# Strassen products that accumulate in PSUM banks, in a two-layer hybrid decoder step

## Chip, core and metric

The kernel runs on one core of a Trainium2 chip. The metric is the device time of one execution in microseconds (us). TensorE multiplies matrices into PSUM banks, VectorE and ScalarE do elementwise work, GpSimd does elementwise work on SBUF alone, and SyncE issues the DMAs. Each engine works through its own queue in order.

## What is computed

One inference step for 512 prompt tokens and 64 sample tokens, through two layers of width 1024. The part that matters here, per layer:

```
h = RMSNorm(x);  P = h @ W_in            # columns: four mixers and four merge-gate blocks G_b
o_b = mixer_b(P_b)                       # HGRN2, GLA, RWKV-7, retention, 256 wide each
x = x + W_out( sum_b sigmoid(G_b) * (o_b @ W_branch[b]) )
g, u = split(RMSNorm(x) @ W_ffn_in)      # 2 x 2816 columns
x = x + (silu(g) * u) @ W_ffn_out
```

Inputs and outputs are float32. The 576 tokens are handled in two halves of 288 (HW). Features lie on the partitions, tokens along the free axis.

## The kernel before

Every float32 operand of a large product is split into two float16 parts, hi and lo. A product of a 128 x 128 weight block with 288 tokens is then three matmuls, hi·hi, hi·lo and lo·hi, into one PSUM bank. To split a weight, ScalarE writes the hi part and VectorE then the lo part (`strassen_weights`, L1692 and L1693; for ordinary products `wload`, L228 and L229).

Two stages use Strassen's scheme in Winograd's form, with seven products of quarter size in place of eight: the merge gates of the last two branches (`last_gates`, eight pairs of feature tiles per layer) and 19 of the 22 feature tiles of the feed-forward's input product (`ffn`, from tile 3 on; one tile of g and one of u together). A is the weight block (rows: two feature tiles; columns: halves of the contraction), B the tokens:

```
S1 = A21 + A22, S2 = S1 - A11, S3 = A22 - S2, S4 = A12 - S2     (GpSimd, L1696)
P1 = A11 B11, P2 = A12 B21, P3 = S4 B22, P4 = A22 T4, P5 = S1 T1, P6 = S2 T2, P7 = S3 T3
U2 = P1 + P6, U3 = U2 + P7, U4 = U2 + P5
C = [[P1 + P2, U4 + P3], [U3 + P4, U3 + P5]]
```

Each product is 12 matmuls (L1718 to L1720), 84 for a tile or a pair. `strassen` (L1708) runs A11, A12, A22, S2, S1, S3, S4, each into a PSUM bank of its own. ScalarE copies P1 to SBUF (L1739). Then seven VectorE additions (L1734), each with one addend in PSUM and one in SBUF, form U2, U4, U3 and the four quarters of C: tiles su and sc. In the feed-forward, ScalarE takes Silu of a quarter of g (L1763), VectorE multiplies it with the quarter of u (L1765, tile fy), and the result is split (L248, L250) into fa. In the merge gates, ScalarE takes Tanh of each quarter (L1529), and after all seven products four up-projections of six matmuls each (tile ub, L1537) follow; VectorE multiplies (L1539, tile gu), GpSimd adds into mg (L1540), and for the last branch mg is split into mh (L252).

The PSUM has eight banks in three rings: b (four), g (two), r (two). A tile of a ring waits until an earlier tile of that ring has had its last reader. During the first four pairs of a layer's merge gates the RWKV-7 recurrence (tiles rws, rtk, ryn, rw_o) runs in between.

The program is written as generators that are stepped in turn; a scheduler then orders the instructions of each engine, and tiles get their memory as they come free. GpSimd works with VectorE on the weights: the sum for S2 needs A11's lo part made first, since it overwrites A11.

Of the kernel before, what the change touches and what calls it, by code (L numbers as in the profile page):

```python
# [62 lines left out]
def host_constants():  # L63
    """Arrays that depend on shapes alone."""
# [110 lines left out]
class Net:  # L175
# [14 lines left out]
    def t(self, ring, shape, name, dt=F32):  # L190
        """A tile of a ring: tiles of one ring get their memory in the program's order."""
# [41 lines left out]
    def gemm(self, ps, w, ks, c0, m, rhs, step=4):  # L233
        """ps[m, :] = sum over k of w(k)^T rhs(k), both in float16 parts. Yields within, after every step products."""
# [10 lines left out]
    def split(self, out_hi, out_lo, src, scale=1.0):  # L245
        """src * scale = hi + lo in float16."""
# [61 lines left out]
    def first_norm(self, half):  # L308
        """x transposed and stored, and its norm, for half the tokens, from the rows of x."""
# [25 lines left out]
    def setup(self):  # L335
        """The other constants."""
# [44 lines left out]
        # lower bounds of HGRN2's forget gates: softmax over depth, cumulated, minus the first  # L381
# [11 lines left out]
        self.lb = cp.tile([128, 2, 2, 2], F32, name="lb")  # [layer, (lb, 1 - lb), tile]  # L393
# [4 lines left out]
        # buffers with zeros off their diagonal blocks that stay  # L398
# [18 lines left out]
    def chunk_sums(self, out, x, mask):  # L417
        """Sums along the tokens that start anew at each chunk's and each sample's first token."""
# [18 lines left out]
    def rstd(self, half):  # L437
        """1 / rms of each token of a half, on all partitions."""
# [50 lines left out]
    def silu_evac(self, dst, scale):  # L489
        """dst = silu(p * PH) * scale."""  # L490
# [1452 lines left out]
```

## Time and profile before

| what | value |
|---|---|
| three runs | 2266.75, 2272.84 (median), 2273.5 us |
| profiled execution, span | 2268.2 us (no other time is listed for it) |
| TensorE busy | 2056.5 us, 91% |
| VectorE busy | 1704.2 us, 75% |
| ScalarE busy | 1070.3 us, 47% |
| GpSimd busy | 693.5 us, 31% |
| merge gates in Strassen's form | about 538 to 692 us, and 1651 to 1805 us |
| feed-forward products in Strassen's form | about 796 to 1009 us, and 1906 to 2121 us |

A share over the whole span is a mean of stages that have different limits, so it is read by stage. The start of a ScalarE copy of P1 (tile sp) marks the end of a tile's first product; the distance between such copies is the period of a tile.

### The profile page before, as it was taken

The page shows a single profiled execution, that of the slowest core. Times are in us where ns is not written, and L with a number is a line of the kernel's source. Part 1 is how long each engine was busy: PE and PEld are TensorE (multiplying, and loading weights), DVE is VectorE, ACT ScalarE, POOL GpSimd, SP SyncE. Part 2 cuts the span into 40 slices and gives each one's busy share as a digit, 9 for nine tenths or more (in the row PEclk, how much of TensorE's full clock was granted, in tenths as well). Part 3 has the DMA queues.
Part 4 walks back from the last instruction along what each step waited for, and adds up shares of the span by engine and source line. Part 5 has one row for each costly group of instructions (what it writes and reads, how often), then busy time and mean ns, then how long its engine had stood idle before and what let it go on. Part 6 is the DMA issues. An engine that isn't in the chain of part 4 may idle for free. (4 is left out here: it accounts for less than half of the span.)

```text
span 2268.2 us, 42128 instructions
## 1 busy us (share of the span) xinstructions
PE 2056.5 (91%) x15754; PEld 1622.1 (72%) x15754; DVE 1704.2 (75%) x3719; ACT 1070.3 (47%) x2400; POOL 693.5 (31%) x850
## 2 busy tenths in 40 slices
PE   7988899997889898999999889889988988989998
PEld 5766776786667676777777667768766766767776
DVE  7899766768786799973388997686688768998532
ACT  6554545346444554442365344363544455444432
POOL 2212212135650555430012121212375416544000
PEclk9999999998999999999999999999999999999999
DMA  6312223322226133234321222242333352232331
GB/s 176 81 36 65 57 57 89 93 72 80 81 80 197 52 88 94 66 117 119 114 71 48 58 54 61 53 111 71 80 88 86 106 155 70 81 89 75 118 109 50
DMA packets 365721, 195.42 MB, mean 86 GB/s; under 512 B 58946, under 2 KB 359546, under 8 KB 365516
## 3 DMA queue, kind: packets, MB, share of 16 engines
q1 hardware_dynamic: 365516, 192.73, 30.3%
q8 instruction: 124, 2.03, 0.4%
q14 instruction: 81, 0.66, 0.1%
HBM read 173.72 MB, written 16.59 MB: 84 GB/s over the span
## 5 line engine op out<-in xcount | busy, mean ns | idle before, releaser
L241 PE MATMUL pb<-h,whl 128*128 128x288 f16 (+1 forms) x1504 | 440.2, 293 | 3.7 <-ACT h L463 2.2
L243 PE MATMUL pb<-h,whl 128*128 128x288 f16 (+1 forms) x1504 | 440.4, 293 | 2.5 <-DVE whl L229 2.5
L242 PE MATMUL pb<-h,whl 128*128 128x288 f16 (+1 forms) x1504 | 440.3, 293 | 0.6 <-DVE h L464 0.4
L229 DVE SCALAR_TENSOR_TENSOR whl<-raw,whl 128x512 f16<-128x512 f32 (+1 forms) x352 | 252.0, 726 | 129.3 <-ACT whl L228 127.6
L242 PEld LDWEIGHTS <-whl 128*128 128x128 f16 (+1 forms) x2784 | 276.9, 99 | 92.0 <-issue 16.1
L243 PEld LDWEIGHTS <-whl 128*128 128x128 f16 (+1 forms) x2784 | 277.4, 100 | 88.8 <-issue 11.9
L241 PEld LDWEIGHTS <-whl 128*128 128x128 f16 (+1 forms) x2784 | 279.3, 100 | 77.1 <-issue 3.6
L228 ACT ACTIVATE whl<-raw 128x512 f16<-128x512 f32 (+1 forms) x352 | 212.8, 616 | 166.7 <-PE pb L243 57.5
L243 PE MATMUL xb<-fa,whl 128*128 128x288 f16 x704 | 201.3, 286 | 0.0
L242 PE MATMUL xb<-fa,whl 128*128 128x288 f16 x704 | 201.3, 286 | 0.0
L241 PE MATMUL xb<-fa,whl 128*128 128x288 f16 x704 | 201.3, 286 | 0.0
L1696 POOL TENSOR_TENSOR sraw<-sraw 128x512 f32<-128x512 f32 x80 | 119.5, 1496 | 70.3 <-DVE hA L1693 34.0
L1718 PE MATMUL fsA<-h,hA 128*128 128x288 f16 x432 | 125.4, 290 | 13.3 <-DVE gu L1539 10.8
L1718 PE MATMUL fsS<-st,hS 128*128 128x288 f16 x456 | 131.3, 288 | 6.4 <-ACT hS L1692 6.4
L1720 PE MATMUL fsS<-st,hS 128*128 128x288 f16 x456 | 131.2, 288 | 0.9 <-DVE hS L1693 0.9
L1719 PE MATMUL fsS<-st,hS 128*128 128x288 f16 x456 | 131.1, 288 | 0.0
L1720 PE MATMUL fsA<-h,hA 128*128 128x288 f16 x432 | 125.4, 290 | 5.1 <-DVE hA L1693 5.1
L1719 PE MATMUL fsA<-h,hA 128*128 128x288 f16 x432 | 125.5, 290 | 0.0
L1696 POOL TENSOR_TENSOR raw<-raw 128x512 f32<-128x512 f32 x52 | 80.1, 1540 | 130.0 <-DVE hA L1693 100.8
L1693 DVE SCALAR_TENSOR_TENSOR hA<-sraw,hA 128x512 f16<-128x512 f32 x110 | 108.2, 992 | 9.8 <-ACT hA L1692 9.7
L1718 PEld LDWEIGHTS <-hS 128*128 128x128 f16 x864 | 85.6, 99 | 34.8 <-ACT hS L1692 12.9
L1719 PEld LDWEIGHTS <-hA 128*128 128x128 f16 x648 | 63.9, 99 | 60.3 <-issue 44.7
(486 smaller groups left out, 5325.4 us busy)
## 6 DMA issues: line engine op xcount, KB each, us to landing
raw<-in_w_in SPq DMA_DIRECT2D x208, 256.0 KB
sraw<-in_w_ffn_in SPq DMA_DIRECT2D x40, 512.0 KB
raw<-in_w_ffn_out SPq DMA_DIRECT2D x80, 256.0 KB
raw<-in_w_ffn_in SPq DMA_DIRECT2D x78, 256.0 KB
x<-xd SPq DMA_DIRECT2D x32, 288.0 KB
sraw<-in_w_in SPq DMA_DIRECT2D x32, 256.0 KB
raw<-in_w_out SPq DMA_DIRECT2D x32, 256.0 KB
xd<-x SPq DMA_DIRECT2D x48, 144.0 KB
```

The lines of the kernel that those rows point to most:

```text
L228: nc.scalar.activation(hl[:, 0, :n], raw[:, :n], AF.Copy, scale=WS)
L229: nc.vector.scalar_tensor_tensor(hl[:, 1, :n], raw[:, :n], WS, hl[:, 0, :n], op0=MUL, op1=SUB)
L241: nc.tensor.matmul(ps, wh, hi, start=i == 0, stop=False)
L242: nc.tensor.matmul(ps, wh, lo, start=False, stop=False)
L243: nc.tensor.matmul(ps, wl, hi, start=False, stop=i == len(ks) - 1)
L1693: nc.vector.scalar_tensor_tensor(hl[:, 1], a, WS, hl[:, 0], op0=MUL, op1=SUB)
L1696: nc.gpsimd.tensor_tensor(dst, a, b, op=op)
L1718: nc.tensor.matmul(ps, w[a][:, 0, k], hi, start=k == 0, stop=False)
L1719: nc.tensor.matmul(ps, w[a][:, 0, k], lo, start=False, stop=False)
L1720: nc.tensor.matmul(ps, w[a][:, 1, k], hi, start=False, stop=k == 3)
```

## The change

P6 and P7 are no longer put into banks of their own. P1 is made in a bank X; ScalarE copies it out as p1, P6 (S2) is accumulated onto it (X is then U2, copied as u2), then P7 (S3; X is U3, copied as u3), and in the next pair's turn P4 (A22; X is then a finished quarter). P5 (S1) is made in a bank Z, and P3 (S4) is accumulated onto it in the next pair's turn. P2 (A12) has a bank Y. Three VectorE additions remain: p1 + Y, u3 + Z, u2 + Z. ScalarE makes three copies, not one. A pair's order is A11, the older pair's A22, S1, the older pair's S4, S2, A12, S3. What follows a quarter (Silu, product and split, or Tanh, up-projection and sum) comes as each quarter is finished. The weights' splits are reordered to suit, and are made further ahead.

```diff
@@ strassen_weights
-        for name, a, op0, op1 in (("A11", a11, a21, a11), ("A22", a22, a22, a11), ("A12", a12, a12, a11)):
-            split(name, a)
-            add(a, op0, op1, SUB)
-            yield
-        for name, a in (("S2", a11), ("S1", a21), ("S3", a22), ("S4", a12)):
-            split(name, a)
-            yield
+        split("A11", a11)
+        add(a11, a21, a11, SUB)
+        yield
+        split("S1", a21)
+        yield
+        split("S2", a11)
+        yield
+        split("A22", a22)
+        add(a22, a22, a11, SUB)
...
@@ strassen
-        def plus(a, p, name):
-            o = self.t(ring if name[1] == "c" else "gt", [128, HW], name)
-            nc.vector.tensor_tensor(o, a, p, op=ADD)
...
-        p1 = self.t("gt", [128, HW], "sp1")
-        nc.scalar.copy(p1, (yield from product("b", "A11", b(0, h0))))
-        c11 = plus(p1, (yield from product("b", "A12", b(4, h0))), "sc11")
-        p4 = yield from product("g", "A22", tt(3))
-        u2 = plus(p1, (yield from product("b", "S2", tt(1))), "su2")
-        p5 = yield from product("g", "S1", tt(0))
-        u4 = plus(u2, p5, "su4")
-        u3 = plus(u2, (yield from product(ps3, "S3", tt(2))), "su3")
-        c22 = plus(u3, p5, "sc22")
-        c21 = plus(u3, p4, "sc21")
-        c12 = plus(u4, (yield from product(ps3, "S4", b(4, h1))), "sc12")
+        def kept(ring, ps, name):
+            o = self.t(ring, [128, HW], name)
+            nc.scalar.copy(o, ps)
+            return o
+        def plus(a, ps):
+            nc.vector.tensor_tensor(a, a, ps, op=ADD)
+            return a
+        old = None
+        for key in [*keys, None]:
+            new = key is not None
+            if new:
+                rx, rz, ry, rc = rings(key)
+                prep(key, 0)
+                x = self.psum(rx, [128, HW], "fsX")
+                yield from product(key, "A11", x, b(0, h0), True)
+                p1 = kept(rc, x, "sp1")
+                prep(key, 1)
+            if old:
+                okey, ox, oz, ou2 = old
+                yield from product(okey, "A22", ox, lambda k: tt(okey, 3, k), False)
+                yield from then(okey, 2, ox)
+            if new:
+                prep(key, 2)
+                z = self.psum(rz, [128, HW], "fsZ")
+                yield from product(key, "S1", z, lambda k: tt(key, 0, k), True)
+                prep(key, 3)
+            if old:
+                yield from product(okey, "S4", oz, b(4, h1), False)
+                yield from then(okey, 1, plus(ou2, oz))
+            if new:
+                prep(key, 4)
+                yield from product(key, "S2", x, lambda k: tt(key, 1, k), False)
+                u2 = kept(rc, x, "su2")
+                prep(key, 5)
+                y = self.psum(ry, [128, HW], "fsY")
+                yield from product(key, "A12", y, b(4, h0), True)
+                yield from then(key, 0, plus(p1, y))
+                prep(key, 6)
+                yield from product(key, "S3", x, lambda k: tt(key, 2, k), False)
+                u3 = kept(rc, x, "su3")
+                yield from then(key, 3, plus(u3, z))
+                old = key, x, z, u2
@@ ffn
+        def then(m, quarter, c):
+            parts[m, quarter] = c
+            if quarter < 2:
+                nc.scalar.activation(c, c, AF.Silu, scale=PH)
+            if quarter in (1, 2):
+                half = 2 - quarter
+                times(m, half, parts.pop((m, half)), parts.pop((m, 2 + half)))
+            return ()
@@ last_gates
+        yield from self.strassen(range(len(pairs)), ..., prep,
+                                 lambda i: ("g", "b" if pairs[i][0] == 2 else "r", "b", "e"), then)
```

The rings are X in g, Y in b, Z in r (in b for the first four pairs of the merge gates).

VectorE's queue in the feed-forward, a stretch of one tile in the middle of the first layer, before. Names are those above; hS and hA are the lo parts of weights.

```order
L1734 TENSOR_TENSOR su_10873<-sp_10804,fsS_10856 128x288
L1693 SCALAR_TENSOR_TENSOR hS_11137<-raw,hS_11137 128x512
L1734 TENSOR_TENSOR su_10892<-su_10873,fsS_10875 128x288
L1693 SCALAR_TENSOR_TENSOR hS_11155<-sraw,hS_11155 128x512
L1734 TENSOR_TENSOR su_10911<-su_10873,fsS_10894 128x288
L1734 TENSOR_TENSOR sc_10913<-su_10911,fsS_10875 128x288
L1734 TENSOR_TENSOR sc_10915<-su_10911,fsA_10840 128x288
L1693 SCALAR_TENSOR_TENSOR hS_11171<-raw,hS_11171 128x512
L1734 TENSOR_TENSOR sc_10934<-su_10892,fsS_10917 128x288
L1765 SCALAR_TENSOR_TENSOR fy<-sc_10915,fsg 128x288
```

The same queue in the changed kernel, 12 of a tile's 14 instructions (L1699 is the lo part of a weight, L1764 an addition, L1813 the product with Silu):

```order
L1813 SCALAR_TENSOR_TENSOR sp_10725<-fsX,sp_10725 128x288
L1699 SCALAR_TENSOR_TENSOR hA_11060<-raw,hA_11060 128x512
L250 TENSOR_TENSOR fa_10877<-sp_10725,fa_10877 128x288
L1699 SCALAR_TENSOR_TENSOR hS_11078<-raw,hS_11078 128x512
L1764 TENSOR_TENSOR su_10804<-su_10804,fsZ 128x288
L1699 SCALAR_TENSOR_TENSOR hS_11096<-raw,hS_11096 128x512
L1813 SCALAR_TENSOR_TENSOR su_10804<-su_10839,su_10804 128x288
L250 TENSOR_TENSOR fa_10877<-su_10804,fa_10877 128x288
L1699 SCALAR_TENSOR_TENSOR hA_11114<-sraw,hA_11114 128x512
L1764 TENSOR_TENSOR sp_10859<-sp_10859,fsY 128x288
L1699 SCALAR_TENSOR_TENSOR hA_11133<-raw,hA_11133 128x512
L1764 TENSOR_TENSOR su_10977<-su_10977,fsZ 128x288
```

Seven additions, of which four came almost together, are now three, spread over the tile; one of the two products with Silu reads the bank X itself.

ScalarE's queue in the feed-forward of the changed kernel (L1698 is the hi part of a weight, L1760 a copy out of X, L1865 Silu):

```order
L1698 ACTIVATE hS_10534<-raw 128x512
L1698 ACTIVATE hS_10552<-raw 128x512
L1865 ACTIVATE su_10260<-su_10260 128x288
L1760 COPY su_10398<-fsX 128x288
L248 ACTIVATE fa_10333<-su_10260 128x288
L1698 ACTIVATE hA_10570<-sraw 128x512
L1698 ACTIVATE hA_10589<-raw 128x512
L1865 ACTIVATE sp_10315<-sp_10315 128x288
L1760 COPY su_10433<-fsX 128x288
```

Two copies out of X stand here behind the hi part of S2 and behind Silu of sums that VectorE makes; before, a tile had one copy.

VectorE's queue in the merge gates, from the end of the sixth pair of the first layer, before (bhl is the lo part of the up-projection's weights):

```order
L1734 TENSOR_TENSOR sc_8166<-su_8164,fsS_8128 128x288
L1734 TENSOR_TENSOR sc_8169<-su_8164,fsA_8093 128x288
L1693 SCALAR_TENSOR_TENSOR hS_8310<-sraw,hS_8310 128x512
L1734 TENSOR_TENSOR sc_8189<-su_8145,fsS_8172 128x288
L1539 SCALAR_TENSOR_TENSOR gu<-sc_8090,ub 128x288
L1693 SCALAR_TENSOR_TENSOR hS_8326<-sraw,hS_8326 128x512
L1539 SCALAR_TENSOR_TENSOR gu<-sc_8166,ub 128x288
L1506 SCALAR_TENSOR_TENSOR bhl<-braw,bhl 128x256
L252 SCALAR_TENSOR_TENSOR mh_8202<-mg_3559,mh_8202 128x288
L1539 SCALAR_TENSOR_TENSOR gu<-sc_8169,ub 128x288
L252 SCALAR_TENSOR_TENSOR mh_8215<-mg_3559,mh_8215 128x288
L1539 SCALAR_TENSOR_TENSOR gu<-sc_8189,ub 128x288
```

And in the changed kernel, the sixth pair's quarters (L1544 is gu):

```order
L1764 TENSOR_TENSOR sp_7963<-sp_7963,fsY 128x288
L1544 SCALAR_TENSOR_TENSOR gu<-sp_7963,ub 128x288
L252 SCALAR_TENSOR_TENSOR mh_8091<-mg_3559,mh_8091 128x288
L1764 TENSOR_TENSOR su_8119<-su_8119,fsZ 128x288
L1699 SCALAR_TENSOR_TENSOR hA_8136<-sraw,hA_8136 128x512
L1544 SCALAR_TENSOR_TENSOR gu<-su_8119,ub 128x288
L252 SCALAR_TENSOR_TENSOR mh_8123<-mg_3559,mh_8123 128x288
L1699 SCALAR_TENSOR_TENSOR hS_8189<-sraw,hS_8189 128x512
L1544 SCALAR_TENSOR_TENSOR gu<-gth,ub 128x288
L1699 SCALAR_TENSOR_TENSOR hS_8205<-sraw,hS_8205 128x512
```

The four products with ub, which came together behind the pair's last addition, now come quarter by quarter, each close behind the addition that its Tanh needs.

## Rows read from the trace of the kernel before

**Rows 1.** Page, part 1: busy time, share of the span, instructions.

```profile
PE 2056.5 (91%) x15754; PEld 1622.1 (72%) x15754; DVE 1704.2 (75%) x3719; ACT 1070.3 (47%) x2400; POOL 693.5 (31%) x850
```

**Rows 2.** Windows, by stage: stretch, length, busy per engine, PEclk, DMA share, GB/s.

```profile
538.00:622.00 84.00, 71.83 (x536) 56.24 (x534) 64.17 (x125) 42.14 (x101) 52.64 (x51) 0.96 0.30 83
632.00:682.00 50.00, 43.72 (x341) 33.84 (x339) 44.37 (x74) 25.38 (x56) 30.25 (x25) 0.97 0.25 74
806.00:938.00 132.00, 118.05 (x953) 92.93 (x952) 131.62 (x200) 64.04 (x135) 67.33 (x45) 1.00 0.30 88
938.00:1009.00 71.00, 67.21 (x546) 52.85 (x544) 63.23 (x115) 32.59 (x73) 27.07 (x19) 1.00 0.25 71
1009.00:1130.00 121.00, 121.00 (x988) 96.57 (x987) 42.87 (x79) 35.83 (x66) 0.00 (x0) 1.00 0.45 133
```

**Rows 3.** Timeline, ScalarE's copies of P1 in the feed-forward: start, length, engine.

```profile
818.43 0.38 ACT L1739 COPY sp<-fsA 128x288 f32<-128x288 f32 x1
...
925.86 0.38 ACT L1739 COPY sp<-fsA 128x288 f32<-128x288 f32 x1
```

**Rows 4.** Waits of TensorE, 796 to 1010: who, for whom, us, times, longest.

```profile
PE fsA L1718 <- DVE sc L1734: 14.0, 10, 1.5
```

**Rows 5.** One line's instructions, VectorE's additions L1734: ns least, median, most.

```profile
L1734 DVE TENSOR_TENSOR su<-su,fsS x108: 437/442/455, 555.1 to 2119.2; 128x288 f32<-128x288 f32 x108
```

**Rows 6.** The same view, lo parts of weights on VectorE, L1693.

```profile
L1693 DVE SCALAR_TENSOR_TENSOR hS<-raw,hS x86: 677/1170/1758, 546.0 to 2104.6; 128x512 f16<-128x512 f32 x86
```

**Rows 7.** The same view, products with Silu on VectorE, L1765.

```profile
L1765 DVE SCALAR_TENSOR_TENSOR fy<-sc,fsg x76: 446/453/1528, 805.6 to 2121.9; 128x288 f32<-128x288 f32 x76
L1765 DVE SCALAR_TENSOR_TENSOR fy<-fb,fsg x12: 443/445/458, 755.4 to 1905.8; 128x288 f32<-128x288 f32 x12
```

**Rows 8.** The same view, GpSimd's sums of weights, L1696.

```profile
L1696 POOL TENSOR_TENSOR sraw<-sraw,raw x50: 1265/1354/1795, 539.7 to 2093.8; 128x512 f32<-128x512 f32 x50
```

**Rows 9.** Timeline, 858 to 862: GpSimd.

```profile
858.35 1.71 POOL L1696 TENSOR_TENSOR sraw<-sraw 128x512 f32<-128x512 f32 x1
860.02 1.72 POOL L1696 TENSOR_TENSOR raw<-raw 128x512 f32<-128x512 f32 x1
```

**Rows 10.** Timeline, 858 to 864: VectorE.

```profile
858.86 1.75 DVE L1693 SCALAR_TENSOR_TENSOR hS<-raw,hS 128x512 f16<-128x512 f32 x1
860.53 0.44 DVE L1734 TENSOR_TENSOR su<-sp,fsS 128x288 f32<-128x288 f32 x1
860.89 1.39 DVE L1693 SCALAR_TENSOR_TENSOR hS<-raw,hS 128x512 f16<-128x512 f32 x1
862.21 0.44 DVE L1734 TENSOR_TENSOR su<-su,fsS 128x288 f32<-128x288 f32 x1
862.57 0.68 DVE L1693 SCALAR_TENSOR_TENSOR hS<-sraw,hS 128x512 f16<-128x512 f32 x1
863.17 0.44 DVE L1734 TENSOR_TENSOR su<-su,fsS 128x288 f32<-128x288 f32 x1
```

**Rows 11.** One line's instructions on ScalarE: hi parts L1692, Silu L1763.

```profile
L1692 ACT ACTIVATE hS<-raw x86: 612/616/632, 539.5 to 2103.6; 128x512 f16<-128x512 f32 x86
...
L1763 ACT ACTIVATE fsg<-sc x76: 425/443/447, 798.8 to 2121.4; 128x288 f32<-128x288 f32 x76
```

**Rows 12.** Timeline, ScalarE's copies of P1 in the merge gates.

```profile
632.34 0.40 ACT L1739 COPY sp<-fsA 128x288 f32<-128x288 f32 x1 [2.45 <-PE fsA L1720]
...
682.26 0.38 ACT L1739 COPY sp<-fsA 128x288 f32<-128x288 f32 x1
```

**Rows 13.** Waits of TensorE, 500 to 690.

```profile
PE fsA L1718 <- DVE gu L1539: 6.3, 4, 2.5
PE xvp L815 <- DVE rws L867: 4.4, 2, 3.4
PE ops L870 <- ACT rtk L811: 3.5, 2, 2.6
```

**Rows 14.** One line's instructions, GpSimd's sums into mg, L1540.

```profile
L1540 POOL TENSOR_TENSOR mg<-mg,gu x64: 784/944/1318, 565.2 to 1802.1; 128x288 f32<-128x288 f32 x64
```

More of the change, by code (lines that the diff above doesn't have):

```diff
@@ L1496, in load, with branch @@
             return a
[L1498 to L1500 removed]
+        wb = {}
+        def branch(i):
+            bi, m = pairs[i][1], pairs[i][3]
+            raw = []
             for k in range(2):
[L1502 to L1503 removed]
+                raw.append(self.t("gt", [128, 256], "braw"))
+                nc.sync.dma_start(out=raw[k], in_=t["w_branch"][l, bi][128 * k:128 * k + 128, 128 * m:128 * m + 256])
+            yield
+            wb[i] = []
+            for a in raw:
@@ new lines, in last_gates, with prep, then @@
+        branches = {}
+        def prep(i, q):
+            self.strassen_prep(gens, i, q)
+            if q == 0:
+                branches[i] = branch(i)
+            if q in (0, 3):
+                next(branches[i])
+        def then(i, quarter, c):
+            q, bi, name, m = pairs[i]
+            j, half = quarter // 2, quarter % 2
+            hs = slice(half * HW, half * HW + HW)
+            th = self.t("e", [128, HW], "gth") if quarter == 2 else c
+            nc.scalar.activation(th, c, AF.Tanh, scale=0.5 * PH)
+            mg = self.mg[m + j]
+            if q == 3 and half == j:
+                self.mh[m + j] = self.t("rs" if m < 6 else "u", [128, 2, T], f"mh{m + j}", F16)
+            ps = self.psum("b", [128, HW], "ub")
+            run(self.gemm(ps, lambda k: wb[i][k], range(2), 128 * j, 128, self.hl_rhs(self.bo[name], half)))
+            u = self.t("e", [128, HW], "gu")
+            nc.vector.scalar_tensor_tensor(u, th, 1.0, ps, op0=ADD, op1=MUL)
+            nc.gpsimd.tensor_tensor(mg[:, hs], mg[:, hs], u, op=ADD)
+            if q == 3:
+                mh = self.mh[m + j]
+                self.split(mh[:, 0, hs], mh[:, 1, hs], mg[:, hs], 0.5 * PA * AS)
+            yield
@@ L1547, in add_x @@
+        yield from self.strassen(range(len(pairs)), lambda i, j, k: [self.T4[2 * j + k // 2][:, k % 2, p] for p in range(2)], prep,
+                                 lambda i: ("g", "b" if pairs[i][0] == 2 else "r", "b", "e"), then)
     def add_x(self, m, half, ps, store, last=False):
@@ new lines, in strassen_weights, with strassen_prep, step @@
+        split("S2", a11)
+        yield
+        split("A22", a22)
+        add(a22, a22, a11, SUB)
+        yield
+        split("A12", a12)
+        add(a12, a12, a11, SUB)
+        yield
+        split("S3", a22)
+        yield
+        split("S4", a12)
+        yield
+    def strassen_prep(self, gens, key, q):
+        def step(k):
+            if k in gens:
+                next(gens[k], None)
+        if q < 4:
+            step(key)
+        if q > 2:
+            step(key + 1)
+        if q == 3:
+            step(key + 2)
@@ L1711, in strassen, with product @@
+    def strassen(self, keys, tt, prep, rings, then):
         nc = self.nc
         h0, h1 = slice(0, HW), slice(HW, T)
-        def product(ring, a, rhs):
-            ps = self.psum(ring, [128, HW], "fs" + a)
+        def product(key, a, ps, rhs, start):
+            w = self.sw[key][a]
             for k in range(4):
                 hi, lo = rhs(k)
-                nc.tensor.matmul(ps, w[a][:, 0, k], hi, start=k == 0, stop=False)
-                nc.tensor.matmul(ps, w[a][:, 0, k], lo, start=False, stop=False)
-                nc.tensor.matmul(ps, w[a][:, 1, k], hi, start=False, stop=k == 3)
+                for i, (part, x) in enumerate(((0, hi), (0, lo), (1, hi))):
+                    nc.tensor.matmul(ps, w[:, part, k], x, start=start and k == i == 0, stop=k == 3 and i == 2,
+                                     skip_group_check=not start)
@@ L1755, in ffn, with times @@
         rings = ["rs"] * 6 + ["gs", "r2"] * 4 + ["gs"] * 2 + ["u"] * 6
-        def gated(m, half, g, u):
+        def times(m, half, sg, u):
             hs = slice(half * HW, half * HW + HW)
@@ L1771, in up @@
                 run(self.gemm(p, w_, range(KT), 0, 128, self.hl_rhs(self.h, half)))
-            gated(m, half, *ps)
+            sg = self.t("e", [128, HW], "fsg")
+            nc.scalar.activation(sg, ps[0], AF.Silu, scale=PH)
+            times(m, half, sg, ps[1])
         def load(m):
@@ L1791, in ffn @@
         self.sw = {}
-        prep = [self.strassen_weights(m, lambda m=m: load(m), "u") for m in range(3, nm)]
-        next(prep[0])
+        prep = {m: self.strassen_weights(m, lambda m=m: load(m), "u") for m in range(3, nm)}
+        next(prep[3])
         for half in range(2):
@@ L1806, in ffn @@
         for _ in range(4):
-            next(prep[0])
-        for m in range(3, nm):
-            if len(prep) > 2:
-                next(prep[2])
-            now, then = prep[0], prep[1] if len(prep) > 1 else None
-            prep.pop(0)
-            def steps():
-                for q in range(7):
-                    if q < 4:
-                        next(now)
-                    if q > 2 and then:
-                        next(then)
-                    yield
-            w = self.sw[m]
-            g0, g1, u0, u1 = result(self.strassen(w, lambda i, k: (T4[i][:, k, 0], T4[i][:, k, 1]), steps(), "r", "gt"))
-            gated(m, 0, g0, u0)
-            gated(m, 1, g1, u1)
+            next(prep[3])
+        parts = {}
+        def then(m, quarter, c):
[6 more added lines that the diff above has]
+            return ()
+        run(self.strassen(range(3, nm), lambda m, i, k: (T4[i][:, k, 0], T4[i][:, k, 1]),
+                          lambda m, q: self.strassen_prep(prep, m, q), lambda m: ("g", "r", "b", "gt"), then))
         def weights(m, rings=("w",)):
```

66 lines of the change are left out of this document (12 added, 54 removed).

## The prediction, made before the changed kernel ran

> **What bounds the kernel now.** I read the page first: TensorE is busy 91% of the span and VectorE 75% [rows 1]. That is a mean over unlike stages, so next come windows by stage [rows 2]. In the stretch 1009 to 1130, the feed-forward's ordinary products, TensorE is busy for all 121.00 us with 988 matmuls: 121.00 / 988 = 0.1225 us for one. A Strassen tile of 84 matmuls can then not be shorter than 84 x 0.1225 = 10.29 us. From 806 to 938, the feed-forward's Strassen products, VectorE is busy 131.62 of 132 us and TensorE 118.05. Nine periods lie between the copies at 818.43 and 925.86 [rows 3]: 107.43 / 9 = 11.94 us a tile. So VectorE sets the pace there, 1.65 us above TensorE's floor, and the waits agree: TensorE stands 14.0 us for VectorE's additions, ten times, until a bank is free [rows 4].
>
> Why is VectorE full? An addition lasts 437 to 455 ns whatever else runs [rows 5]; a lo part takes 677 to 1758 [rows 6]; a product with Silu 446 to 1528 if both factors lie in SBUF and 443 to 458 if they lie in PSUM and SBUF [rows 7]. The timeline shows when: while GpSimd works at 858.35 and 860.02 [rows 9], the lo parts at 858.86 and 860.89 last 1.75 and 1.39, the addition between them 0.44, and the lo part at 862.57, with GpSimd idle, 0.68 [rows 10]. Records overlap a little, so I count from start to start: 0.36 for an addition (860.53 to 860.89) and 0.60 for a free lo part (862.57 to 863.17). A tile before has seven lo parts and eleven shorter instructions (seven additions, two products, two lo parts of fa): 7 x 0.60 + 11 x 0.36 = 8.16 us. The rest, 11.94 - 8.16 = 3.8 us, is waiting for GpSimd's four sums, 0.94 each.
>
> In the merge gates neither engine is full. From 632 to 682, TensorE is busy 43.72 of 50 us and VectorE 44.37 [rows 2]; three periods take 682.26 - 632.34 = 49.92, 16.64 each [rows 12], against 108 matmuls x 0.1225 = 13.23. TensorE waits there for gu, 6.3 us in four waits: all four banks of ring b hold up-projections when the next pair wants one [rows 13]. In the first four pairs it waits for the recurrence too (4.4 and 3.5).
>
> **Part by part: the feed-forward.** Four additions a tile go, 4 x 0.36 = 1.44 us of VectorE. One product with Silu now reads X in PSUM, hence takes 0.36 always. Left are 14 instructions: 7 x 0.60 + 7 x 0.36 = 6.72. The waits for GpSimd do not shrink in step. The four additions that go are of the kind that never waited; they were work VectorE could do while GpSimd ran. I followed one tile through the new queue with GpSimd's sum at its shortest, 1.27 [rows 8]. The sum for S2 starts behind A11's lo part and fa's and holds up S1's lo part 1.25; the next tile's sum for S1 holds up S2's 0.9; those for S3 and S4 hold up A12's and S3's 0.9 each: 4.0 in all. Once a tile VectorE also stands 0.5 for ScalarE's hi part of fa, which follows its product directly. Sum: 6.72 + 4.0 + 0.5 = 11.2 us. From below the period is bounded by TensorE's 10.29; from above by four whole sums, 6.72 + 5.1 + 0.5 = 12.3, which is longer than now. I take 11.2, since the 4.0 is near the 3.8 read before. Eleven periods of the stretch gain 11 x (11.94 - 11.2) = 8.1. In its tail, 938 to 1009, TensorE idles 71.00 - 67.21 = 3.8; of that I take 1.5, because the weights of A22 and S4 now hold their places in ring u one tile longer, where fa's last six tiles take places too (0 to 3.8 either way). That is 9.6 a layer. The two layers' stages are equally long (213 and 215 us), so 19 us.
>
> The Trainium skill, "SBUF — State Buffer", section "Who interferes with whom", states the rule behind these rows: a VectorE instruction with two SBUF inputs and a GpSimd one that reads SBUF exclude each other, one blocking fully, while one SBUF input does not contend. The trace agrees (0.44 beside GpSimd, 1.75 against 0.68). It speaks against this change: without it, time would fall with the number of instructions, 11.94 x 14 / 18 = 9.3, and TensorE would be the bound, the second case below; with it 11.2 is what is left.
>
> **ScalarE, banks, loads.** ScalarE gets two more copies of 0.38 [rows 3], 0.76 a tile on an engine that is busy 64.04 of 132 us [rows 2]; its load is no bound. The new wait is: S3 may not go into X until u2 has been copied out, S2 not until p1, A22 not until u3. For p1 there are three products of room (4.4 us), for u3 one product (1.5), and behind the last pair none (0.6, once a stage). For u2 there is one product, and its copy is queued behind S2's hi part, which waits for GpSimd, and behind a Silu, which waits for VectorE. Counted from the end of the older A22: product 0.36, A11's lo part 0.60 to 1.32, GpSimd 1.27 to 1.71, hi part 0.62, Silu 0.44 [rows 11], copy 0.38, together 3.7 to 4.8, against four products, 4 x 12 x 0.1225 = 5.9, before S3's turn comes. So I cost it at nothing; it makes TensorE follow VectorE's pace, which the 11.2 holds already. Loads are now issued in the fourth step of the tile two before; their buffers come free by S4's split at that step before as well, so nothing starts later. If one is late, GpSimd's first sum is, which is needed most of a tile later.
>
> **Merge gates.** The four up-projections no longer come together, and ring b serves fewer tiles, so the wait for gu goes. What is late next is VectorE. Pairs 5 to 8: seven lo parts, and thirteen short ones (three additions, four gu, four mh, two halves of bhl): 7 x 0.60 + 13 x 0.36 = 8.9. GpSimd's weight sums cost 4.0 as above. Each gu now stands close behind the addition whose Tanh it needs, and each mh behind a gu that goes through GpSimd (0.94, [rows 14]) and ScalarE (0.44): about 0.5 once and 1.0 twice that nothing hides, 2.5. Sum 15.4, gain 1.2 x 4 = 4.8 (bounds: 13.23, and 16.64 or more). Pairs 1 to 4: TensorE idles 84.00 - 71.83 = 12.2 [rows 2]; 7.9 of that is the recurrence's and stays; of the other 4.3 I take 2.5. That is 7.3 a layer, 15 us for two.
>
> **Sum.** 19.2 + 14.6 = 34 us. The profiled execution's span is 2268.2, so 2234.4 for the span; the median of the runs, 2272.8, lies 4.6 above it: 2239.
>
> **The rivals.** TensorE becomes the bound. For: its floor is below all the sums above, and GpSimd may find gaps in which VectorE waits anyway. Against: the rows on exclusion. Feed-forward 11 x (11.94 - 10.3) + 3 = 21 a layer; gates 4 x (16.64 - 13.6) + 4 = 16; together 75: 2198.
>
> No gain in the feed-forward: the time in which GpSimd keeps VectorE out grows to near 4.7 us a tile, as the additions beside it are gone. The period stays at 11.9, and the gates give half, 7 us: 2266.
>
> Slower, by ScalarE's queue: if VectorE runs behind as it does now, the copy of u2 is late, S3 waits in TensorE's in-order queue, and A11 and A22 of the next turn with it, and VectorE's u3 + Z waits for S3 in turn. The chain may take 5.9 + 1.65 = 7.5 before the period passes 11.94, so this decides from a backlog of some 2.7 us. At 0.6 over, 38 tiles cost 23 and the gates give nothing: 2296. For it: before, TensorE waited 1.5 for a bank because of such a backlog. Against it: VectorE's work falls.
>
> **How the numbers follow.** Forecast 0.60, TensorE as bound 0.17, no gain in the feed-forward 0.15, slower 0.08. A measurement tells some 0.3%, 7 us, from no change. Faster: the first two and 0.06 of the third, 0.83. Same: 0.08 of the third and 0.01 of the fourth, 0.09. Slower: 0.01 and 0.07, 0.08. The range takes in most of the second case and the third: 2200 to 2264. The forecast's own range, with a period from 10.8 to 11.6, is 2222 to 2256.
>
> **What would show it.** Right: in the middle of the feed-forward stage a period near 11.2, VectorE still over 95% busy or held by GpSimd and ScalarE, TensorE some 92% busy; in gate pairs 5 to 8 a period near 15.4 and no waits for gu before A11. A period near 10.3 with TensorE at 100% proves the first rival; waits of S3 for a ScalarE copy, with a period above 11.9, the last. If the waits of lo parts for GpSimd sum to less than 3 us a tile, my count of them is wrong.

## The result, and the profile after

The changed kernel takes 2304.07 us (median of four runs, 2303.73 to 2305.22); the kernel before took 2273.17 in the same comparison. The ratio of the runs is 1.0151, 95% interval 1.0134 to 1.0167 (the two medians alone stand at 1.0136, inside it): slower by more than the noise, where 34 us less was forecast and a range of 2200 to 2264. Its profiled execution has a span of 2302.3 us against 2268.2.

First the page's line of busy time [rows 1], whole span:

```profile
PE 2066.3 (90%) x15754; PEld 1623.7 (71%) x15754; DVE 1608.2 (70%) x3503; ACT 1113.1 (48%) x2508; POOL 669.8 (29%) x850
```

VectorE has 96 us less work than before, as the removed additions promise, and the kernel is longer all the same. So VectorE doesn't bound it any more; the stages show what does. The columns are those of [rows 2]; the stretches lie a little later than before, since the kernel runs behind.

```profile
535.00:632.00 97.00, 85.00 (x620) 65.67 (x619) 74.22 (x127) 52.02 (x125) 61.79 (x58) 0.95 0.34 91
632.00:705.00 73.00, 59.76 (x459) 45.77 (x457) 41.15 (x75) 30.41 (x69) 26.35 (x26) 0.95 0.30 91
800.00:945.00 145.00, 127.14 (x999) 98.36 (x999) 113.07 (x165) 78.14 (x168) 63.85 (x48) 0.99 0.29 84
```

In the feed-forward VectorE is busy 113.07 of 145 us, 78%, where it was over 99% before, and TensorE 88%, where it was 89%. All engines have room, and the stage still takes longer: something waits in a chain. The copies of P1 give the period [rows 3]:

```profile
821.14 0.38 ACT L1760 COPY sp<-fsX 128x288 f32<-128x288 f32 x1
...
931.75 0.38 ACT L1760 COPY sp<-fsX 128x288 f32<-128x288 f32 x1
```

Nine periods lie between: (931.75 - 821.14) / 9 = 12.29 us, against 11.94. Where the time went, by marks on TensorE (first matmul of a stage, before and after): the start of the first out-projection, behind the merge gates, moves from 691.45 to 694.48 (+3.0). The feed-forward, from its first product to its output product, goes from 263.8 to 274.0 (+10.3). From there to the end of the second layer's merge gates it is 791.0 before and 804.8 after (+13.8), for the second feed-forward 263.2 and 269.4 (+6.2). The second out-projection gives 2.9 back, and what follows the second feed-forward takes 3.1 more. So both stages lose, in about equal parts. TensorE's waits, whole span, largest first [rows 4, 13]:

```profile
PE fsX L1750 <- ACT su L1760: 76.3, 66, 3.9
PE xvp L815 <- DVE rws L867: 31.7, 15, 4.4
...
PE fsX L1750 <- ACT sp L1760: 5.9, 2, 3.0
```

The waits for a bank (sc) and for gu are gone, as forecast; those for the recurrence (rws) grow from 24.3 to 31.7 us. TensorE now waits 76.3 us, 66 times, until ScalarE has copied u2 or u3 out of X. In 800 to 945 it does so 18 times, 15.3 us in all; every second tile has a wait of 1.8 us or more. The timeline shows the longest of these:

```profile
896.93 1.63 PE L1750 MATMUL fsX<-st,hS 128*128 128x288 f16 x12
...
898.78 0.45 DVE L1764 TENSOR_TENSOR su<-su,fsZ 128x288 f32<-128x288 f32 x1
899.35 1.26 POOL L1702 TENSOR_TENSOR raw<-raw,sraw 128x512 f32<-128x512 f32 x1 [3.97 <-DMA raw<-in_w_ffn_in]
...
900.58 1.26 POOL L1702 TENSOR_TENSOR sraw<-sraw 128x512 f32<-128x512 f32 x1
901.87 0.63 ACT L1698 ACTIVATE hS<-sraw 128x512 f16<-128x512 f32 x1 [3.73 <-POOL sraw L1702]
902.41 0.43 ACT L1865 ACTIVATE su<-su 128x288 f32<-128x288 f32 x1
902.53 0.69 DVE L1699 SCALAR_TENSOR_TENSOR hS<-sraw,hS 128x512 f16<-128x512 f32 x1 [3.31 <-ACT hS L1698]
902.74 0.38 ACT L1760 COPY su<-fsX 128x288 f32<-128x288 f32 x1
...
903.17 1.02 PE L1750 MATMUL fsX<-st,hS 128*128 128x288 f16 x7 [3.13 <-ACT su L1760]
```

S2 has run into X by 898.56 (896.93 + 1.63). The copy could go then, and goes at 902.74. Ahead of it in ScalarE's queue stand a hi part of a weight sum and a Silu; the hi part waits for GpSimd's sum at 900.58, which stands in GpSimd's queue behind a sum of a later tile that waits 3.97 us for a load. The Silu's own input was ready at 899.2. VectorE, idle, waits 3.31 us for the same hi part. This is ScalarE's queue at such a place, as the program orders it (a plain list of its instructions; su_11076 is one tile's u2, hS_11216 and hS_11234 are S1 and S2 of the tile after next):

```
L248 ACTIVATE fa_11015<-sp_10859 128x288
L1698 ACTIVATE hS_11216<-sraw 128x512
L1698 ACTIVATE hS_11234<-sraw 128x512
L1865 ACTIVATE su_10942<-su_10942 128x288
L1760 COPY su_11076<-fsX 128x288
```

In TensorE's queue the S2 of the tile after next comes fourteen products after this tile's S2, and this tile's S3 two products after it. A copy that is needed in one product's time thus stands behind work that is needed two tiles later. In the merge gates the same copy stands behind another stranger:

```profile
654.33 0.45 DVE L1764 TENSOR_TENSOR sp<-sp,fsY 128x288 f32<-128x288 f32 x1
654.81 0.44 ACT L1537 ACTIVATE sp<-sp 128x288 f32<-128x288 f32 x1 [1.12 <-DVE sp L1764]
655.29 0.46 DVE L1544 SCALAR_TENSOR_TENSOR gu<-sp,ub 128x288 f32<-128x288 f32 x1 [0.51 <-ACT sp L1537]
655.82 0.79 POOL L1545 TENSOR_TENSOR mg<-mg,gu 128x288 f32<-128x288 f32 x1 [3.13 <-DVE gu L1544]
656.64 0.44 ACT L248 ACTIVATE mh<-mg 128x288 f16<-128x288 f32 x1 [1.39 <-POOL mg L1545]
656.99 0.38 ACT L1760 COPY su<-fsX 128x288 f32<-128x288 f32 x1
...
657.43 2.80 PE L1750 MATMUL fsX<-mt,hA 128*128 128x288 f16 x11 [3.85 <-ACT su L1760]
```

An addition, a Tanh, a product on VectorE, a sum on GpSimd and the hi part of mh run one after the other, and the copy of u3, which needs none of them, comes last. TensorE stands for 3.85 us.

### The profile page after: what moved, and what is told of

The parts are those of the page before. It is cut to its first block, busy times and chain, and to the rows that moved or that the text cites. A ratio compares the mean times of both kernels' runs of the same rounds, so it can differ in the third digit from the quotient of the medians.

```text
span 2302.3 us, 42094 instructions
## 1 busy us (share of the span) xinstructions
PE 2066.3 (90%) x15754; PEld 1623.7 (71%) x15754; DVE 1608.2 (70%) x3503; ACT 1113.1 (48%) x2508; POOL 669.8 (29%) x850
## 5 line engine op out<-in xcount | busy, mean ns | idle before, releaser
L1750 PEld LDWEIGHTS <-hS 128*128 128x128 f16 x2592 | 256.1, 99 | 134.0 <-issue 62.9
L242 PEld LDWEIGHTS <-whl 128*128 128x128 f16 (+1 forms) x2784 | 276.5, 99 | 89.9 <-issue 14.4
L1750 PEld LDWEIGHTS <-hA 128*128 128x128 f16 x1944 | 193.9, 100 | 85.5 <-issue 33.3
L1750 PE MATMUL fsX<-st,hS 128*128 128x288 f16 x912 | 126.1, 289 | 42.7 <-ACT su L1760 36.8
L1699 DVE SCALAR_TENSOR_TENSOR hS<-sraw,hS 128x512 f16<-128x512 f32 x130 | 117.6, 909 | 60.6 <-ACT hS L1698 57.2
L1702 POOL TENSOR_TENSOR sraw<-sraw 128x512 f32<-128x512 f32 x80 | 108.4, 1355 | 130.4 <-DVE hA L1699 87.3
L1698 ACT ACTIVATE hS<-sraw 128x512 f16<-128x512 f32 x130 | 80.5, 625 | 88.4 <-POOL sraw L1702 88.2
L1699 DVE SCALAR_TENSOR_TENSOR hA<-sraw,hA 128x512 f16<-128x512 f32 x110 | 106.6, 974 | 7.8 <-ACT hA L1698 5.9
L1702 POOL TENSOR_TENSOR raw<-raw 128x512 f32<-128x512 f32 x52 | 70.1, 1347 | 100.3 <-DVE hA L1699 78.3
L1103 ACT ACTIVATE le<-le 128x128 f32<-128x128 f32 (+2 forms) x124 | 43.9, 354 | 113.5 <-DVE le L1102 109.7
L430 ACT ACTIVATE sq<-x 128x288 f32<-128x288 f32 x64 | 28.1, 438 | 140.4 <-DVE x L1556 140.2
L1699 DVE SCALAR_TENSOR_TENSOR hS<-raw,hS 128x512 f16<-128x512 f32 x86 | 84.5, 984 | 12.0 <-ACT hS L1698 9.5
```

Source lines behind the costliest of these rows:

```text
L242: nc.tensor.matmul(ps, wh, lo, start=False, stop=False)
L430: nc.scalar.activation(sq, self.x[k][:, hs], AF.Square)
L1103: nc.scalar.activation(E, E, AF.Exp)
L1698: nc.scalar.activation(hl[:, 0], a, AF.Copy, scale=WS)
L1699: nc.vector.scalar_tensor_tensor(hl[:, 1], a, WS, hl[:, 0], op0=MUL, op1=SUB)
L1702: nc.gpsimd.tensor_tensor(dst, a, b, op=op)
```

## The experiments

Every kernel was compared with the kernel before, run beside it; ratios are compared, not medians. `issue_after(x)` forbids the scheduler to queue what stands in it ahead of x on that engine; it adds no wait. The scheduler then orders the rest anew, so an edit for one engine can move the instructions of others. `self.copied` is the copy out of X that was last in the program's order. "Period" is the mean of nine feed-forward periods, as above; "waits" are TensorE's for copies su, whole span.

| run | ratio (95% interval) | period | waits |
|---|---|---|---|
| changed kernel | 1.0151 (1.0134 to 1.0167) | 12.29 | 76.3, 66 times |
| e1 feed-forward alone | 1.0080 (1.0057 to 1.0104) | 12.17 | 43.4, 47 |
| e2 gates alone | 1.0066 (1.0047 to 1.0084) | 11.94 | 30.7, 17 |
| e3 GpSimd's order | 1.0079 (1.0060 to 1.0097) | 11.61 | 61.5, 46 |
| e5 mh's split later | 1.0125 (1.0096 to 1.0154) | 12.21 | 68.4, 63 |
| e6 earlier loads | 1.0169 (1.0128 to 1.0210) | 12.28 | 84.5, 71 |
| e9 Silu behind the copy | 1.0094 (1.0073 to 1.0114) | 11.49 | 61.4, 37 |
| e10 S2's hi part behind | 1.0116 (1.0100 to 1.0132) | 11.92 | 74.9, 55 |
| e7 = e3 + e5 | 1.0045 (1.0032 to 1.0058) | 11.60 | 54.8, 48 |
| e12 = e7 + e9 + S2, S4 behind | 0.9936 (0.9911 to 0.9962) | 11.53 | 46.3, 40 |
| e15 = e12 + quarter 0 behind u3 | 0.9886 (0.9850 to 0.9922) | 11.53 | 39.9, 34 |
| e13 = e15 + all hi parts behind | 0.9776 (0.9741 to 0.9811) | 10.81 | 24.6, 41 |
| e14 = e13 without e3 and e5 | 0.9927 (0.9903 to 0.9951) | 11.18 | 39.3, 47 |

In e14 periods of 10.2 and 12.4 us alternate, so nine of them flatter it; ten give 11.29.

**Which stage.** e1 and e2 put the old scheme back in one stage each (`strassen_o` is `strassen` of the kernel before).

```diff
@@ e1, last_gates
-        yield from self.strassen(range(len(pairs)), lambda i, j, k: [self.T4[2 * j + k // 2][:, k % 2, p] for p in range(2)], prep,
-                                 lambda i: ("g", "b" if pairs[i][0] == 2 else "r", "b", "e"), then)
+            c = yield from self.strassen_o(self.sw[i], lambda j, k: [self.T4[2 * j + k // 2][:, k % 2, p] for p in range(2)],
...
@@ e2, ffn
-        run(self.strassen(range(3, nm), lambda m, i, k: (T4[i][:, k, 0], T4[i][:, k, 1]),
...
+            g0, g1, u0, u1 = result(self.strassen_o(w, lambda i, k: (T4[i][:, k, 0], T4[i][:, k, 1]), steps(), "r", "gt"))
```

> Only the feed-forward has the changed scheme; the merge gates are those of before. By the marks in the two traces (first out-projection, first feed-forward tile, last Strassen tile) the changed feed-forward costs about 10 us a layer, so theory A (each stage loses by itself, in its own way) expects 2273 + 20 = 2293 us, 2287 to 2299. Rival: the loss is made in the gates and only shows in the feed-forward, because its loads and weights begin later; then the time is within 7 us of before, 2266 to 2280, and the period of a feed-forward tile is 11.9 us, not 12.3.

> Only the merge gates have the changed scheme; the feed-forward is that of before. Theory A: pairs 1 to 4 gain some 3 us a layer, pairs 5 to 8 lose some 9, together +14 for two layers less what the earlier start hides: 2273 + 14 = 2287 us, 2279 to 2293. Rival: the gates' loss is the feed-forward's loads taking their place in SyncE's queue; then 2266 to 2277.

2287.42 and 2283.74 us. 0.80% and 0.66% add to 1.46%, against 1.51% for both: each stage loses by itself, and in e2 the feed-forward's period is that of before.

**GpSimd's queue and mh's split.**

```diff
@@ e3, strassen_weights (sum4: the sum for S4 of the tile before)
-        add(a21, a21, a22, ADD)
+        if ring == "u" and self.sum4:
+            with self.tc.issue_after(self.sum4.ins):
+                add(a21, a21, a22, ADD)
@@ e5, then in last_gates
+            if late:
+                with self.tc.issue_after(self.copied.ins):
+                    late.pop()()
...
-                self.split(mh[:, 0, hs], mh[:, 1, hs], mg[:, hs], 0.5 * PA * AS)
+                late.append(lambda: self.split(mh[:, 0, hs], mh[:, 1, hs], mg[:, hs], 0.5 * PA * AS))
```

> The changed kernel, but in the feed-forward GpSimd's first sum for a tile (into S1) is queued behind the fourth sum (into S4) of the tile before it, so that a late load can't stand ahead of the sum for S2. Theory B (late load, then GpSimd's queue, then the hi part of S2 in ScalarE's queue, then the copy of u2, then S3 on TensorE): the 3 us waits of S3 for that copy go in half of the tiles, the period falls from 12.29 to about 11.3 us, 19 tiles a layer, 2 layers: about -30 at most, 2275 to 2292 us in all. Rival C (VectorE, held by GpSimd, is the limit, and the copies are merely late with it): the period stays at 12.2 to 12.4 and the time at 2300 to 2308. Rival D (the load itself is what is late, wherever the sum stands): the wait moves to the first sum and S1, period above 12.

> The changed kernel, but in the merge gates each split of mg into mh is issued a quarter later, with its hi part queued on ScalarE behind the latest copy out of X. Theory E (the copy out of X stands in ScalarE's queue behind mh's hi part, which waits for GpSimd's sum into mg, which waits for gu): the waits of TensorE for su in 640 to 720 us, 10.6 us in six, fall to 2 or less, and the two layers gain about 7 each: 2304 - 14 = 2290 us, 2285 to 2297. Rival F (pairs 5 to 8 are slow because VectorE is late with sp and gu; the copy follows anyway): waits for su are replaced by waits for something of VectorE, and the time stays within 4 us of 2304.

e3: 2286.65 us. The waits of 3 us in the feed-forward are gone, the longest before a copy of u2 or u3 is now 1.1 us in 800 to 945, and the period is 11.61, below that of before. This is theory B's direction, though the period stops short of 11.3; rivals C and D are out. By the two programs' instruction lists e3 changes GpSimd's queue alone, so half of the loss goes without a change to ScalarE's queue. e5: 2298.78 us, just above theory E's range. The gate pairs' periods in the first layer fall from 19.8, 17.0, 20.6 to 16.5, 18.5, 16.6, but the six waits fall only from 10.6 to 7.8 us, not to 2: the copy still stood behind a Tanh there. Its interval overlaps that of the changed kernel, so the gain rests on the periods more than on the time.

> The changed kernel with both reorderings: GpSimd's first sum behind the fourth of the tile before (feed-forward) and mh's splits a quarter later (gates). If the two losses are independent the gains add: 17 + 5 = 22 us, 2280 to 2284 us. Rival: the stage that begins earlier waits for the same loads as before and gives back some: 2284 to 2290.

2276.28 us: 1.0045, so 1.06% below the changed kernel; e3 and e5 alone gave 0.72% and 0.26%. They add.

**The load.**

```diff
@@ e6, pools and ffn's load
-        self.wp = pool("wraw", 4)
+        self.wp = pool("wraw", 5)
-            for o in (0, DFF):
+            for o in (DFF, 0):
-            return q
+            return q[2:] + q[:2]
```

> The changed kernel with its orders, but one more buffer for loaded weights (five, not four), and the even feed-forward tiles load the quarters that GpSimd's first sum needs first. If the late load is the start of the loss in the feed-forward, GpSimd's 4 us waits for the transfer fall to 1 or 2 and half of S3's 3 us waits go: 2288 to 2298 us. Rival (the load is not the start; the sum only stands where it would be late anyway): 2300 to 2308 us.

2305.61 us: nothing gained, my theory of the load fell. GpSimd's waits in 800 to 945, of the changed kernel and of e6:

```profile
POOL sraw L1702 <- DVE hA L1699: 31.2, 16, 4.7
POOL sraw L1702 <- DMA sraw<-in_w_ffn_in: 17.2, 6, 3.8
POOL raw L1702 <- DVE hA L1699: 17.0, 9, 2.9
POOL raw L1702 <- DMA raw<-in_w_ffn_in: 13.7, 4, 4.0
```

```profile
POOL sraw L1702 <- DVE hA L1699: 42.2, 18, 4.9
POOL raw L1702 <- DVE hA L1699: 18.3, 12, 2.4
POOL raw L1702 <- DMA raw<-in_w_ffn_in: 15.2, 5, 3.1
POOL sraw L1702 <- DMA sraw<-in_w_ffn_in: 4.3, 6, 1.3
```

Its waits for transfers fall from 30.9 to 19.5 us, by a third and not to nothing, and those for VectorE's lo parts rise from 48.2 to 60.5. With that link of the chain shorter, GpSimd waits as long for the next. Late loads are not new either; the kernel before has them in the same stretch, with no copy behind them that TensorE needs at once:

```profile
POOL raw L1696 <- DMA raw<-in_w_ffn_in: 16.9, 4, 5.1
```

**ScalarE's queue, piece by piece.** In e9 the Tanh of the gates is treated as the Silu; every Silu and Tanh, and not that of u2 + Z alone, is queued behind the copy that stands last before it in the program, and in the gates the up-projections move on TensorE too. e12 and e15 name S2 and S4 in the line of e10, e13 and e14 all seven weights.

```diff
@@ e9, strassen (then: Silu and product, or Tanh, up-projection and sum)
-                yield from then(okey, 1, plus(ou2, oz))
+                oc = plus(ou2, oz)
...
                 u2 = kept(rc, x, "su2")
+            if old:
+                yield from then(okey, 1, oc)
@@ e9, then
+                with self.tc.issue_after(self.copied.ins):
+                    nc.scalar.activation(c, c, AF.Silu, scale=PH)
@@ e10, strassen_weights, split
+            if self.copied and name in ("S2",):
+                with self.tc.issue_after(self.copied.ins):
+                    nc.scalar.activation(hl[:, 0], a, AF.Copy, scale=WS)
@@ e15, strassen
-                yield from then(key, 0, plus(p1, y))
+                c11 = plus(p1, y)
...
                 u3 = kept(rc, x, "su3")
+                yield from then(key, 0, c11)
```

> The changed kernel, but S2's hi part on ScalarE is queued behind the copy out of X that stands last before it in the program's order; in the changed kernel the hi part of S2 of the tile after next stands ahead of this tile's copy of u2. GpSimd's queue stays as it is. Theory B (the copy is late because of what is queued ahead of it): S3's 3 us waits for su go although the load and GpSimd's sum are as late as before, period 12.29 to 11.6 us or less, 2284 to 2292 us in all. Rival C2 (it is GpSimd's order that costs, by holding VectorE and the weights; the copy only shows it): the period stays above 12 and the time above 2298.

> The changed kernel, but what follows the quarter u2 + Z (Silu or Tanh) is queued on ScalarE behind the next copy of u2, and in the merge gates the up-projection of that quarter stands behind S2 on TensorE. Theory G (part of the copy's delay is the Silu or Tanh that waits for VectorE's addition): S3's waits of 1 us in every other feed-forward tile go, 0.4 us a tile, and one wait of up to 3 us per pair in the gates: 2292 to 2299 us. Rival: S3 waits just as long for its own lo part of VectorE then, or for S2's hi part that still stands ahead: within 4 us of 2304.

e10: 2293.26 us, outside the 2284 to 2292 of theory B. By the ratios it gains 0.35%, 8 us, where 12 to 20 were expected, and its period of 11.92 lies between the two theories. The 3 us wait is gone, but S3 still waits 0.99 us at 895.53, since the copy stands behind a Silu and a hi part of fa that wait for VectorE, and TensorE's waits for su in 800 to 945 come to 15.1 us, as in the changed kernel. Nor did GpSimd's queue stay as it was: the scheduler put the sum for S2 ahead of the first sum that waits for a load. So e10 doesn't separate theory B from rival C2.

e9: 2287.00 us, better than expected: the feed-forward's period falls by 0.8 us, twice what I counted. TensorE's queue in the feed-forward is that of the changed kernel, and GpSimd's too but for the stage's end. The first sum still waits there for its load ahead of the sum for S2:

```profile
888.91 1.28 POOL L1703 TENSOR_TENSOR raw<-raw,sraw 128x512 f32<-128x512 f32 x1 [3.32 <-DMA raw<-in_w_ffn_in]
890.15 1.26 POOL L1703 TENSOR_TENSOR sraw<-sraw 128x512 f32<-128x512 f32 x1
```

So in the feed-forward the place of the Silu on ScalarE, with the few instructions of VectorE that moved with it, is enough to bring the period below the 11.94 of the kernel before.

> As the run before it, and further the Silu or Tanh of the quarter u2 + Z and the hi parts of S2 and S4 are queued on ScalarE behind the copy out of X. If ScalarE's queue ahead of the copies is what is left of the loss, the feed-forward's period comes to 11.0 to 11.4 us and gate pairs 5 to 8 to 15.5 to 16.5 us: 2255 to 2272 us, and faster than the kernel before. Rival (VectorE, held by GpSimd, and the chain of splits are the limit by now): period 11.6 as in the first reordering, 2278 to 2284 us.

> As the run with S2 and S4 behind the copies, and further what follows the quarter p1 + Y (Silu or Tanh) is queued on ScalarE behind the copy of u3, for which the older A22 there still waits 1.08 us in each feed-forward tile. If ScalarE's order is still what costs, half a microsecond a tile or more comes back: period 11.0 us or less, 2232 to 2245 us. Rival (VectorE's own work and its waits for hi parts set the 11.5 us, the copy's wait is only slack used up): period 11.4 to 11.6, 2248 to 2256 us.

e12: 2251.42 us, faster than the kernel before, with a longer period than I had expected (11.53, not 11.4 or less). e15: 2242.31 us, in the range of the theory, but by luck: its feed-forward's period did not move, as the rival said, and the gates' did (first layer, last four: 17.5, 16.4, 15.2, 14.4 against 17.9, 16.2, 16.6, 15.5). The intervals of e12 and e15 overlap.

> As the run before it, but all seven hi parts of a tile's weights, not S2's and S4's alone, are queued behind the copy out of X that stands last before them in the program's order. Theory: no wait of TensorE for a copy above 0.5 us is left, period 10.8 to 11.2 us as the prediction counted for VectorE, 2230 to 2245 us. Rival: the weights then come so late that TensorE waits for their lo parts instead; period 11.5 or more, 2250 to 2275 us.

> The same queueing of ScalarE's work behind the copies as in the run before, but GpSimd's sums and mh's splits in the order of the changed kernel. If ScalarE's order alone is the cause of the loss, this is faster than the kernel before: 2235 to 2262 us. Rival: GpSimd's first sum, waiting for its load ahead of the sum for S2, still makes weights late and VectorE idle: 2265 to 2285 us.

e13: 2217.48 us, below its 2230 to 2245, with a period inside its range; it is 2.2% faster than the kernel before and, by the ratios, 3.7% faster than the changed one. TensorE's waits for copies come to 5.2 us in 800 to 945, none above 0.75; in the gates one of 3.3 is left. Its page, and its windows in the feed-forward and at the end of the merge gates:

```profile
PE 2049.3 (92%) x15754; PEld 1620.9 (73%) x15754; DVE 1572.1 (71%) x3503; ACT 1108.3 (50%) x2508; POOL 686.2 (31%) x850
```

```profile
800.00:945.00 145.00, 139.81 (x1126) 109.78 (x1124) 115.71 (x191) 87.90 (x191) 76.61 (x53) 1.00 0.33 97
640.00:690.00 50.00, 45.66 (x372) 36.19 (x370) 39.27 (x64) 26.52 (x61) 22.81 (x20) 1.00 0.37 114
```

TensorE is busy 96% of the feed-forward stretch, and ScalarE does the same work as in the changed kernel, in another order. Its timeline, at S2, the copy and S3:

```profile
884.03 1.63 PE L1765 MATMUL fsX<-st,hS 128*128 128x288 f16 x12
884.43 1.72 POOL L1713 TENSOR_TENSOR raw<-raw,sraw 128x512 f32<-128x512 f32 x1
...
884.93 0.45 DVE L1832 SCALAR_TENSOR_TENSOR sp<-fsX,sp 128x288 f32<-128x288 f32 x1
...
885.30 1.39 DVE L1710 SCALAR_TENSOR_TENSOR hS<-sraw,hS 128x512 f16<-128x512 f32 x1
...
886.28 0.38 ACT L1775 COPY su<-fsX 128x288 f32<-128x288 f32 x1
...
886.97 1.63 PE L1765 MATMUL fsX<-st,hS 128*128 128x288 f16 x12
...
888.06 0.44 ACT L1887 ACTIVATE su<-su 128x288 f32<-128x288 f32 x1 [1.40 <-DVE su L1779]
```

The copy goes 0.6 us after S2's end at 885.66, the Silu that waits 1.40 us for VectorE comes behind it, and S3 starts without a wait.

e14 takes e3's and e5's edits away again: 2248.53 us, in its range and faster than the kernel before. The queueing behind the copies is worth 2.24% (1.0151 to 0.9927), more than the whole loss of 1.51%; on top of it e3's and e5's edits give another 1.5%. But e14 is not ScalarE's order alone. In the gates TensorE's up-projections move with the Tanh, and in the feed-forward the scheduler changed GpSimd's queue too: in 14 tiles of the two layers the changed kernel has the first sum of the next tile ahead of the sum for S2 (899.35 and 900.58 above), and e14 has the sum for S2 ahead:

```profile
889.31 1.27 POOL L1708 TENSOR_TENSOR sraw<-sraw 128x512 f32<-128x512 f32 x1 [2.77 <-issue]
890.55 1.49 POOL L1708 TENSOR_TENSOR raw<-raw,sraw 128x512 f32<-128x512 f32 x1
```

So its rival, that a first sum in that place keeps the kernel slow, was not put to the test by it. What the runs show together: the loss lies in the order of the queues that lead to the copy. In the feed-forward GpSimd's order alone (e3) or the Silu's place alone (e9) each takes the period below that of before; in the gates mh's place (e5) takes 5.8 us off three periods of the first layer; and the copies put first (e14) more than undo the loss. How it divides between ScalarE's queue and GpSimd's is not shown. Not tried: what the same queueing would give the kernel before.

## Why the prediction was wrong

**The step that failed** is "ScalarE, banks, loads", which I cost at nothing. The place was right: "its copy is queued behind S2's hi part, which waits for GpSimd, and behind a Silu, which waits for VectorE". The chain I counted there, 3.7 to 4.8 us against four products of room, has GpSimd's sum at its bare length, 1.27 to 1.71 us, as if GpSimd were free when its inputs are. It is not: its queue held a sum that waited 3.97 us for a load. I had that too, and let it go: "If one is late, GpSimd's first sum is, which is needed most of a tile later". The first sum is needed late; the sum queued behind it holds up the copy. And I took the weights in ScalarE's queue for those of the tile at hand. The order shows that they are two tiles ahead: the copy waited for work with no hurry. In place of nothing, the runs showed 76.3 us of waits for the copies of u2 and u3, and 1.5% more time.

**The rival that came true** was the one at 0.08: waits of S3 for a ScalarE copy, with a period above 11.9. Its 2296 us was 8 too low: it priced the feed-forward at 23 us and the gates at nothing, where e1 and e2 give 0.80% and 0.66%, 18 and 15 us, so that its sum is near by luck. What decided was not a backlog of VectorE, as I wrote; VectorE was idle 22% of the stage.

**The gates.** The waits for gu went, as forecast. The chain of addition, Tanh, gu, GpSimd and mh was in the sum, with 2.5 us "that nothing hides", but on VectorE's account. Its cost fell on the copy behind mh in ScalarE's queue, and so on TensorE: three periods from 621.56 to 678.93, 19.1 us each, not 15.4. Pairs 1 to 4 gained more than the 2.5 us that I took: from the first pair's copy of P1 to the fifth's it is 81.97 us, 89.69 before.

**The feed-forward's 11.2 us** on VectorE could not be seen in the changed kernel, whose VectorE had time to spare. e13 shows it mis-sized as well, in the other direction: 10.81. By the prediction's own test (less than 3 us of lo parts waiting for GpSimd) the term of 4.0 us was wrong. In 820 to 930 of the changed kernel, lo parts on VectorE (columns: busy us, mean ns, idle before):

```profile
L1699 DVE SCALAR_TENSOR_TENSOR hS<-sraw,hS 128x512 f16<-128x512 f32 x23 | 23.1, 1005 | 17.7 <-ACT hS L1698 17.0
L1699 DVE SCALAR_TENSOR_TENSOR hA<-sraw,hA 128x512 f16<-128x512 f32 x18 | 18.4, 1022 | 0.5
L1699 DVE SCALAR_TENSOR_TENSOR hS<-raw,hS 128x512 f16<-128x512 f32 x13 | 12.6, 972 | 1.0 <-ACT hS L1698 0.2
L1699 DVE SCALAR_TENSOR_TENSOR hA<-raw,hA 128x512 f16<-128x512 f32 x9 | 9.8, 1091 | 0.0
```

63 lo parts take 63.9 us, 1.01 each, 0.33 above the free 0.68: 7 x 0.33 = 2.3 us a tile. In e13 72 of them take 61.1 us in the same stretch: 0.85 each, 1.2 us a tile; the product with Silu that has both inputs in SBUF adds 0.4 there. Where VectorE must wait for ScalarE's hi parts anyway (17.0 us here), GpSimd's sums run in those gaps: by the records of 820 to 930, 13.9 of GpSimd's 47.2 us fall where VectorE is idle, 22.5 of 59.3 in e13, and none of 56.2 in the kernel before. The first rival, TensorE as the bound, had named such gaps; with the queues put right the kernel comes to 0.9776 x 2272.8 = 2222 us, at the lower edge of the forecast's own range and 24 above that rival's 2198. The exclusion itself stands: in e13 the lo part at 885.30 lasts 1.39 beside a sum of GpSimd, and the product with an addend in PSUM at 884.93 only 0.45. The Trainium skill, "SBUF — State Buffer", section "Who interferes with whom", says the same of two SBUF inputs and of one; the trace agrees, and it was my count of overlaps that was too high.

## What to carry to other kernels

When a reader of PSUM takes over the part of freeing an accumulator, it becomes part of TensorE's path; look up what stands ahead of it in its own engine's queue, and in the queues that those wait for, before costing it at nothing. An engine half idle can still be the bound by its order: copies that TensorE needs soon belong ahead of splits that are needed tiles later. In a chain of waits, shortening one link (the load) may give nothing, and reordering another much. And look at every engine's queue after an edit to one: the scheduler may have moved what the experiment was to hold still.

## What was not expected of the hardware

A wait can cost more than its length. TensorE was idle for 2.37 us up to 649.74 in the merge gates and for 3.85 us up to 657.43; after the second wait the granted clock is 0.50, the lower of its two levels (1.2 GHz), in 657.4 to 661:

```profile
657.40:661.00 3.60, 3.57 (x16) 2.18 (x16) 1.59 (x4) 1.48 (x4) 2.02 (x2) 0.50 0.00 0
661.00:665.00 4.00, 4.00 (x26) 2.84 (x25) 3.71 (x6) 3.01 (x8) 1.18 (x1) 0.76 0.22 66
```

Its twelve matmuls take 3.04 us, where twelve take 1.63 at the full clock: 1.4 us on top of the wait, and the next ones are slow too. Over 640 to 690 the granted clock is 0.93, against 0.97 in the kernel before and 1.00 in e13. Not every such wait does this. In e14 the clock falls after 3.02 us of waiting up to 661.21 (0.58 in 661 to 665), but in e13 it is 1.00 after 3.30 us up to 655.73, and in the changed kernel after the 3.13 us up to 903.17:

```profile
903.00:910.00 7.00, 6.61 (x53) 5.15 (x53) 6.28 (x10) 4.41 (x10) 2.54 (x2) 1.00 0.00 0
```

Nor is the clock what makes the kernel slower as a whole: over the span it is 0.970, against 0.971 before.
